# Loading all of x first, 1/rms through TensorE transposes, and padded stationaries by GpSimd, in a two-layer hybrid attention kernel

## The chip, the cores and the metric

One core of one Trainium2 chip runs the kernel in one launch. The metric is the device time of an execution in microseconds (us), the median of several runs. TensorE (PE; its weight loads are PEld), VectorE (DVE), ScalarE (ACT), GpSimd (POOL) and SyncE (SP, which here issues every DMA) each work through a queue of their own in order, and wait for one another by semaphores. TensorE has two clock levels, 1.2 and 2.4 GHz; the profile gives the granted share, 1.00 being the higher.

## The reference, cut to what matters

Two layers over 16 learned meta tokens and 1024 tokens of width 1024, all in float32. Each layer computes from u = RMSNorm(h) one projection u @ w_in, and from it two attention groups:

```
u = rms_norm(h, norm_g)
dq, dk, dv, dz, fq, fk, fv, fz, f_logit = split(u @ w_in)
# four differential heads: two softmaxes of 64-wide q and k with rope, one 128-wide v
p   = softmax(q1 k1^T / 8) - lam * softmax(q2 k2^T / 8)          # causal
o_a = rms_norm(p @ v_a, subln_g) * (1 - lambda_init)              # norm over the 128 of a head
# eight FoX heads of 64: softmax(q k^T / 8 + c_q - c_k), c = cumsum(log_sigmoid(f_logit + b))
o_b = p_f @ v_f
h   = h + concat(o_a * silu(dz), o_b * silu(fz)) @ w_out
```

After the second layer comes a last RMSNorm, and the meta rows are dropped. The norm over a head (rms_norm with subln_g) is what sub_norm below computes.

## The kernel before, in words

**Numbers.** Float32 products are made of float32r pairs: a value is split into a high part (rounded) and a low part (the rest), so that a product takes three matmuls (high x high, low x high, high x low). XTh and XTl hold u transposed in that form; load_w (lines 289 to 313) loads a column of 128 of w_in in four pieces of 128 KB and lets GpSimd make both parts (lines 307 and 310).

**Order of the work.** First all of x is normalised and transposed (lines 926 to 958). Then, for each layer, eight units j run one after another, four differential and then four FoX units of two heads each: unit_proj projects k, q and v (proj, line 334, in three chunks of about 346 tokens), attend makes scores, probabilities and outputs block by block of 128 queries, unit_gate projects z and multiplies. The projection of unit j+1 is written after the attention of unit j, before sub_norm(j) and the gates. The output projection (line 1049) closes a layer. Every pool of tiles is a set of buffers that the planner assigns: it takes the program as written, works out an order for each engine's queue from its own estimates of duration, places all tiles in memory and adds the waits, those for the reuse of memory included. Where a pool gives no count, the planner chooses it.

**The start.** Block 0 is the 16 meta rows, blocks 1 to 8 are 128 tokens each; they are loaded in the order 1, 0, 2, 3, ..., and after the fourth of them (W0 = 3) the four pieces of the first weight column are loaded. Groups of blocks, (1), (0, 2), (3, 4), (5, 6), (7, 8), are normalised: squares on ScalarE with a row sum, the chain of rsqrt on VectorE (lines 221 to 238, a start value and three Newton steps), and then rms_apply, x * r * g on VectorE (line 260), transposes on TensorE (line 275), a copy to XTh on ScalarE and the rest to XTl on VectorE (line 286). Blocks 5, 6 and 7 (PG) go another way: GpSimd multiplies by g alone (line 954), and a matmul against a diagonal of r scales and transposes at once (line 277).

**Differential units.** A block of 128 queries has two softmaxes, m = 0 and 1, over the two halves of the 128 partitions. The low part of the queries is used against both halves of k in one matmul, so it needs a stationary whose other half is zero: low_queries (lines 647 to 656) copies the half it needs, 64 partitions by 128, into one of two zeroed buffers qz by a DMA (named XTl<-ql in the trace, since the buffers lie in XTl's tile), two for each block, 68 blocks in all. finish_o leaves in U.vr the sums of squares of the outputs. sub_norm (lines 888 to 902) makes 1/rms of them in U.vr[:, 1], one column for each block of queries, one row for each query, while the outputs OT have queries along the free axis. So it writes the columns to DRAM (rr), loads them back as a row sent to all partitions (bc), and multiplies:

```
dma(row[NM:].rearrange("(b p) -> p b", p=P), U.vr[:, 1, 1:9])
bc = st("bc")
dma(bc[:, tq:], bcast_rows(row[tq:], P))
nc.vector.scalar_tensor_tensor(out=OT[:, tq:], in0=OT[:, tq:], scalar=gsc[...], in1=bc[:, tq:], ...)
```

Of the kernel before, what the change touches and what calls it, by code (L numbers as in the profile page):

```python
# [12 lines left out]
F32 = mybir.dt.float32  # L13
# [6 lines left out]
P = 128  # L20
NM = 16
# [6 lines left out]
PADC = (272, 544, 1056)  # L28
CSW = 1060
# [6 lines left out]
ECL = ((272, 4),)  # L36
# [4 lines left out]
W0 = 3  # L41
ON_POOL = ()
SPL_POOL = ()
GRPS = ((1,), (0, 2), (3, 4), (5, 6), (7, 8))
# [8 lines left out]
VPB = 2  # L53
STB = 3
NQZ = 2
PMB = 4
OTB = 2
CKB2 = 2
# [20 lines left out]
PG = (5, 6, 7)  # L79
# [37 lines left out]
def hybrid_kernel(ctx: ExitStack, tc: tile.TileContext, x, meta, norm_g, w_in, b_forget,  # L117
# [12 lines left out]
    sm = ctx.enter_context(tc.tile_pool(name="sm", bufs=6))  # L130
# [27 lines left out]
    def et(name, w=L):  # L158
        for i, (wmax, nb) in enumerate(ECL):
            if w <= wmax:  # L160
                return big.tile([P, wmax], F32, name=name, tag=f"es{i}" if i else "es", bufs=nb or None)
        return big.tile([P, LE], F32, name=name, tag="e", bufs=NE or None)
# [5 lines left out]
    cst = const.tile([P, max(CSW, P + 96 + MW // 2)], F32, name="cst")  # L168
# [21 lines left out]
    rr = [[dr.tile([L], F32, name=f"rr{i}_{j}") for j in range(4)] for i in range(DEPTH)]  # L190
# [50 lines left out]
    def rms_stats(hbs, junk, eng):  # L241

        ss = sm.tile([P, 4, 4], F32, name="ss", tag="ss", bufs=3)
# [19 lines left out]
    def put_ut(b, u, on_pool=False, r=None):  # L263

        t0, n = blk(b)
        if r is not None:
            dg = ptp.tile([P, P], F32, name="dg", tag="pm")
            nc.vector.tensor_scalar(out=dg[:n, :n], in0=ident[:n, :n], scalar1=r[:n], scalar2=None, op0=ALU.mult)
# [75 lines left out]
    def load_v01(l):  # L344
# [4 lines left out]
        wf = wp.tile([P, KT, 8], F32, name="wf", tag="wf", bufs=1)  # L349
# [16 lines left out]
    def proj_v01(l, his, los):  # L366
        Vs = [vp.tile([P, NB, 2, P], F32R, name="V", tag="V") for _ in range(2)]
        Vms = [vp.tile([96, 2, P], F32R, name="Vm", bufs=2) for _ in range(2)]
        vpre[l] = (Vs[1], Vms[1])

        mm = big.tile([P, 384], F32R, name="mm", tag="ck", bufs=CKB2 or None).rearrange("p (k c) -> p k c", k=KT)
# [8 lines left out]
        vm = big.tile([P, 384], F32, name="vm", tag="ck", bufs=CKB2 or None)[0:NM, :NV]  # L380
# [8 lines left out]
        fn = sm.tile([P, 8, NB], F32, name="fn", tag="fn", bufs=1)  # L389
        fm = sm.tile([NM, 8], F32, name="fm", tag="fm", bufs=1)  # L390
# [23 lines left out]
    def forget(l):  # L414
# [49 lines left out]
    def unit_proj(l, j, U, tabs):  # L464
# [113 lines left out]
        Vm = vp.tile([96, 2, P], F32R, name="Vm", bufs=2)  # L578

        def evv(ps, t0, n):  # L580
            vr = big.tile([P, 384], F32, name="vr", tag="ck", bufs=CKB2 or None)
            nc.scalar.activation(vr[:, :n], ps[:, :n], AF.Copy, scale=1.0 if diff else 0.5)
            late.append(lambda: transpose_v(vr, t0, n))
# [44 lines left out]
    def unit_gate(l, U, from_dram):  # L628
# [9 lines left out]
        def evz(ps, t0, n):  # L638
            gt = big.tile([P, 384], F32, name="gt", tag="ck", bufs=CKB2 or None)
# [7 lines left out]
    def low_queries(U, t):  # L647

        if not U.diff:
            return [U.Qb[m][:, t:t + P] for m in range(2)]  # L650
        qz = qzs[nqz[0] % NQZ]
        nqz[0] += 1
        for m in range(2):
            h = slice(64 * m, 64 * m + 64)
            dma(qz[h, m, :], U.ql[h, t:t + P])
        return [qz[:, m, :] for m in range(2)]

    def scores(U, m, i, low):
# [7 lines left out]
        s = sm.tile([P, 8], F32, name="sst", tag="sst", bufs=SSB or None)  # L666
# [93 lines left out]
    def split_meta(U, ps, n):  # L760
        pm = ptp.tile([96, 256], F32R, name="pm")
# [21 lines left out]
    def attend_meta(U):  # L783

        s = sm.tile([P, 8], F32, name="sst", tag="sst", bufs=SSB or None)
# [102 lines left out]
    def sub_norm(U):  # L888
# [84 lines left out]
    for l in range(DEPTH):  # L973
# [78 lines left out]
        def out_open(b):  # L1052
# [8 lines left out]
            ss = sm.tile([P, 4, 4], F32, name="ss", tag="ss", bufs=3)  # L1061
# [100 lines left out]
```

## Time and profile before

| | |
|---|---|
| median of three timed runs | 1522.74 us (1522.72 to 1524.1) |
| the profiled execution | 1519.45 us, span 1517.7 us from its first to its last instruction |
| TensorE / its weight loads busy | 1426.1 us (94%) / 1353.4 us (89%) |
| VectorE, ScalarE, GpSimd busy | 966.1 (64%), 697.7 (46%), 581.4 us (38%) |
| mean granted clock of TensorE | 0.975 |
| DMA | 128.37 MB, mean 85 GB/s |

A profile shows one execution. An engine's busy time counts the instructions, not its waits; a wait is put down to whatever released it last. Rows of a timeline give the start, the length, the engine and line, what is written from what is read, and in brackets how long the engine was idle before and what ended that. SPq rows are SyncE's DMA issues, not the transfers.

### The profile page before, as it was taken

What the parts mean: (1) busy time and instruction counts of PE and PEld (TensorE: products, weight loads), DVE (VectorE), ACT (ScalarE), POOL (GpSimd) and SP (SyncE); (2) the same over time, 40 slices, a digit from 0 to 9 for tenths busy, and PEclk for the clock granted to TensorE, in tenths of its full rate; (3) what the DMA queues carried; (4) which work ended last, traced back from release to release, by engine and by line L of the source; (5) the groups of instructions that cost most, each with busy time, mean ns of one, the idle gap of its engine ahead of it and who ended that gap; (6) DMA issues with size and microseconds to landing.
All of it is one profiled execution on the core that took longest, in us unless ns stands there. A gap on an engine that the chain in (4) does not pass through costs nothing.

```text
span 1517.7 us, 26880 instructions
## 1 busy us (share of the span) xinstructions
PE 1426.1 (94%) x9218; PEld 1353.4 (89%) x9218; DVE 966.1 (64%) x2729; ACT 697.7 (46%) x1729; POOL 581.4 (38%) x985
## 2 busy tenths in 40 slices
PE   3999988989899999999999998989898999999997
PEld 3998878989899999997789998889798999999886
DVE  6558684948465756575655686677566466756653
ACT  4236443626444655465323554445344455555521
POOL 6514243523344444464005233343333454535500
PEclk7999999999999999999999999999999999999999
DMA  8325232444133324356424244233433223244632
GB/s 191 66 51 76 33 96 47 87 55 93 25 101 65 62 50 65 93 148 183 135 102 96 40 68 73 55 76 64 61 70 81 68 50 82 45 83 122 208 132 84
DMA packets 132761, 128.37 MB, mean 85 GB/s; under 512 B 26192, under 2 KB 112336, under 8 KB 132624
## 3 DMA queue, kind: packets, MB, share of 16 engines
q1 hardware_dynamic: 132624, 126.65, 38.2%
q8 instruction: 73, 1.20, 0.3%
q14 instruction: 64, 0.52, 0.1%
HBM read 75.15 MB, written 21.57 MB: 64 GB/s over the span
## 4 chain that ended last, share of the span: by engine, by line
PE 69%; DMA 11%; DVE 10%; issue 4%; ACT 3%; POOL 2%; SPq 1%; DVEq 0%; ACTq 0%; POOLq 0%
PE pj L334 34%; PE pss L1049 4%; PE pj L1049 4%; DMA wraw<-in_w_in_dram 3%; PE pss L671 3%; PE pss L673 3%; PE pt L846 3%; PE pj L399 3%; PE po L780 2%; PE po L781 2%; DVE E L677 2%; DMA hb<-in_x_dram 1%; DMA bc<-rr 1%; DVE k L501 1%; PE po L778 1%
## 5 line engine op out<-in xcount | busy, mean ns | idle before, releaser
L334 PE MATMUL pj<-XTh,whi 128*128 128x346 f32 (+5 forms) x1392 | 456.4, 331 | 15.4 <-POOL whi L307 13.6
L334 PE MATMUL pj<-XTl,whi 128*128 128x346 f32 (+5 forms) x1392 | 454.5, 327 | 6.0 <-DVE XTl L286 6.0
L334 PE MATMUL pj<-XTh,wlo 128*128 128x346 f32 (+5 forms) x1392 | 455.5, 328 | 1.7 <-POOL wlo L310 1.7
L684 ACT ACTIVATE E<-E,sst 128x144 f32<-128x144 f32 (+7 forms) x256 | 202.1, 790 | 197.0 <-DVE sst L677 185.3
L334 PEld LDWEIGHTS pj<-XTh,whi 128*128 128x128 f32 x1392 | 265.6, 192 | 19.6 <-POOL whi L307 15.5
L334 PEld LDWEIGHTS pj<-XTl,whi 128*128 128x128 f32 x1392 | 266.1, 191 | 7.4 <-DVE XTl L286 6.4
L334 PEld LDWEIGHTS pj<-XTh,wlo 128*128 128x128 f32 x1392 | 266.5, 192 | 4.5 <-POOL wlo L310 3.6
L307 POOL TENSOR_SCALAR whi<-wraw 128x256 fp32r<-128x256 f32 x232 | 110.1, 475 | 346.4 <-DMA wraw<-in_w_in_dram 315.6
L310 POOL TENSOR_TENSOR wlo<-wraw,whi 128x256 fp32r<-128x256 f32 x232 | 181.0, 781 | 114.8 <-PE pj L334 97.7
L755 DVE TENSOR_TENSOR ptl<-pt,pth 128x512 fp32r<-128x512 f32 (+1 forms) x240 | 147.4, 633 | 52.5 <-ACT pth L754 47.0
L671 PE MATMUL pss<-k,qa 128*128 128x400 f32 (+7 forms) x448 | 154.1, 347 | 10.7 <-DVE sst L677 8.6
L754 ACT CAST pth<-pt 128x512 fp32r<-128x512 f32 (+1 forms) x240 | 122.7, 546 | 85.0 <-PE pt L846 29.8
L677 DVE CUSTOM_DVE_ANT_0 E<-pss,cst 128x400 f32<-128x400 f32 (+7 forms) x256 | 123.9, 491 | 40.6 <-PE pss L673 34.2
L701 POOL TENSOR_SCALAR E<-E,sst 128x400 f32<-128x400 f32 (+7 forms) x128 | 97.2, 762 | 136.2 <-DVE sst L700 121.2
L677 DVE CUSTOM_DVE_ANT_0 E<-pss,cst,sst 128x264 f32<-128x264 f32 (+2 forms) x192 | 112.1, 584 | 36.9 <-PE pss L673 31.9
L671 PEld LDWEIGHTS pss<-k,qa 128*128 128x128 f32 x448 | 86.0, 192 | 16.9 <-DVE sst L677 13.2
L846 PE MATMUL pt<-cst,E 128*128 128x128 f32 x576 | 89.8, 274 | 0.5 <-DVE sst L677 0.5
L780 PE MATMUL po<-pth,V 128*128 128x256 f32 x320 | 84.0, 286 | 0.6 <-POOL pth L865 0.6
L781 PE MATMUL po<-ptl,V 128*128 128x256 f32 x320 | 82.7, 287 | 0.0
L673 PE MATMUL pss<-k,XTl 128*128 128x400 f32 (+6 forms) x224 | 73.4, 334 | 4.0 <-DMA XTl<-ql 4.0
L494 POOL TENSOR_TENSOR sw<-sw,sin 128x694 f32<-128x694 f32 (+3 forms) x32 | 50.1, 1570 | 65.0 <-DMA sw<-raw 51.3
L673 PE MATMUL pss<-k,q 68*128 68x400 f32 (+6 forms) x224 | 72.8, 328 | 0.0
(337 smaller groups left out, 2881.3 us busy)
## 6 DMA issues: line engine op xcount, KB each, us to landing
wraw<-in_w_in_dram SPq DMA_DIRECT2D x256, 128.0 KB
hb<-in_x_dram SPq DMA_DIRECT2D x16, 512.0 KB
wor<-in_w_out_dram SPq DMA_DIRECT2D x64, 128.0 KB
XTl<-ql SPq DMA_DIRECT2D x136, 32.0 KB
sw<-raw SPq DMA_DIRECT2D x48, 86.8 KB
ms<-OT SPq DMA_DIRECT2D x8, 520.0 KB
k<-k SPq DMA_DIRECT2D x16, 260.0 KB
h<-hb SPq DMA_DIRECT2D x8, 512.0 KB
```

Of the source, the lines that this page charges most:

```text
L310: nc.gpsimd.tensor_tensor(out=lo, in0=raw, in1=hi.bitcast(F32), op=ALU.subtract)
L334: nc.tensor.matmul(ps[:, :n], lhsT=w, rhs=xx[:, k, t0:t0 + n], start=(cnt == 0), stop=(cnt == 23))
L671: nc.tensor.matmul(ps[:, :nn], lhsT=U.Qa[m][:, t:t + P], rhs=U.K1[m][:, c0:c0 + nn], start=True, stop=False)
L673: nc.tensor.matmul(ps[:, :nn], lhsT=low[m], rhs=U.Kb[m][:, c0:c0 + nn], start=False, stop=True)
L677: nc.vector.tensor_tensor_reduce(out=E[:, c0:c0 + n], in0=ps[:, :n], in1=k, scale=-1.0, scalar=s[:, c - 1:c] if CHN and c else -NEG, op0=A ...
L684: nc.scalar.activation(E[:, :W], E[:, :W], AF.Exp, scale=-1.0, bias=lo, accum_out=s[:, 4:5])
L754: nc.scalar.copy(hi, ps)
L755: nc.vector.tensor_tensor(out=lo, in0=ps, in1=hi.bitcast(F32), op=ALU.subtract)
L780: nc.tensor.matmul(o[:, :256], lhsT=U.V[:, kb, hd, :], rhs=hi, start=False, stop=False)
L781: nc.tensor.matmul(o[:, :256], lhsT=U.V[:, kb, hd, :], rhs=lo, start=False, stop=last)
L846: nc.tensor.transpose(ps[:, (2 * a + b) * P:(2 * a + b + 1) * P], PP[:, k0:k0 + P], ident)
L1049: nc.tensor.matmul(ps, lhsT=xx[:, k, m0:m0 + P], rhs=wo[k][w][:, c], start=(k == 0 and i == 0), stop=(k == KT - 1 and i == 2))
```

## The change

Five things are changed at once.

1. The start: the first weight column is loaded after all nine blocks of x (W0 = 8); the groups are (0, 1, 2), (3, 4, 5), (6, 7, 8); PG is empty, so every block goes through rms_apply on VectorE and plain transposes.
2. sub_norm: no DRAM. For each block of queries TensorE transposes the column of 1/rms spread over 128 columns (a broadcast operand), which gives a PSUM tile with the row in every partition; VectorE multiplies from there, four blocks at a time.
3. low_queries: a GpSimd copy (multiplication by one) instead of the DMA, into one of three buffers instead of two.
4. The pool sm and the tags es, ck and subn go: their tiles become rings at fixed places in the tile cst, with as many slots as there were buffers, handed out in the order of the program. Two tiles mm move to the tag pth.
5. Paddings: PADC 264, 528, 1056, 2112 (264 is the quarter of 1056), some tiles widened from 96 or 16 to 128 partitions; the number of buffers of the pool of V is left to the planner (VPB = 0).

```diff
-PADC = (272, 544, 1056)
-CSW = 1060
+PADC = (264, 528, 1056, 2112)
-W0 = 3
+W0 = 8
-GRPS = ((1,), (0, 2), (3, 4), (5, 6), (7, 8))
+GRPS = ((0, 1, 2), (3, 4, 5), (6, 7, 8))
-VPB = 2
+VPB = 0
-NQZ = 2
+NQZ = 3
-PG = (5, 6, 7)
+PG = ()
...
-    sm = ctx.enter_context(tc.tile_pool(name="sm", bufs=6))
...
+    small = [("es", 4, 272), ("ck", 2, 384), ("subn", 2, 36), ("sst", SSB, 8), ("ss", 3, 16), ("fn", 1, 64), ("fm", 1, 8), ("wf", 1, 64)]
+    cst = const.tile([P, P + 96 + MW // 2 + sum(n * w for _, n, w in small)], F32, name="cst")
+    rings, at = {}, P + 96 + MW // 2
+    for nm, n, w in small:
+        rings[nm] = [at, n, w, 0]
+        at += n * w
+
+    def slot(nm):
+        r = rings[nm]
+        c = r[0] + r[3] % r[1] * r[2]
+        r[3] += 1
+        return cst[:, c:c + r[2]]
...
-            dma(qz[h, m, :], U.ql[h, t:t + P])
+            nc.gpsimd.tensor_scalar(out=qz[h, m, :], in0=U.ql[h, t:t + P].bitcast(F32), scalar1=1.0, scalar2=1.0,
+                                    op0=ALU.mult, op1=ALU.mult)
...
-        row = rr[U.l][U.j]
-        if U.l == 0:
-            dma(row[0:NM].rearrange("(p b) -> p b", b=1), U.vr[0:NM, 1, 0:1])
-        dma(row[NM:].rearrange("(b p) -> p b", p=P), U.vr[:, 1, 1:9])
-        bc = st("bc")
-        dma(bc[:, tq:], bcast_rows(row[tq:], P))
-        nc.vector.scalar_tensor_tensor(out=OT[:, tq:], in0=OT[:, tq:], scalar=gsc[:, U.l, U.j:U.j + 1],
-                                       in1=bc[:, tq:], op0=ALU.mult, op1=ALU.mult)
+        for t0, n, cols in ((0, NM, (0,)), (NM, 4 * P, (1, 2, 3, 4)), (NM + 4 * P, 4 * P, (5, 6, 7, 8))):
+            if t0 < tq:
+                continue
+            ps = pt()
+            w = min(n, P)
+            for i, c in enumerate(cols):
+                nc.tensor.transpose(ps[:, w * i:w * i + w], U.vr[0:w, 1, c:c + 1].to_broadcast([w, P]), ident[0:w, 0:w])
+            o = OT[:, t0:t0 + n]
+            nc.vector.scalar_tensor_tensor(out=o, in0=o, scalar=gsc[:, U.l, U.j:U.j + 1], in1=ps[:, :n],
+                                           op0=ALU.mult, op1=ALU.mult)
```

## Rows read from the trace of the kernel before

**Rows 1.** The page, busy time by engine.

```profile
PE 1426.1 (94%) x9218; PEld 1353.4 (89%) x9218; DVE 966.1 (64%) x2729; ACT 697.7 (46%) x1729; POOL 581.4 (38%) x985
```

**Rows 2.** Windows by stage: length, PE, PEld, DVE, ACT, POOL busy (count), clock, DMA, GB/s.

```profile
97.00:430.00 333.00, 302.74 (x1944) 287.10 (x1943) 226.86 (x670) 155.34 (x407) 120.65 (x193) 0.96 0.36 66
430.00:850.00 420.00, 418.43 (x2712) 393.32 (x2711) 255.03 (x721) 196.03 (x491) 166.16 (x295) 1.00 0.40 95
850.00:1157.00 307.00, 280.25 (x1832) 269.76 (x1831) 211.14 (x595) 145.06 (x358) 110.01 (x181) 0.97 0.38 68
```

**Rows 3.** Windows of the first 20 us.

```profile
0.00:10.00 10.00, 6.68 (x44) 6.49 (x45) 3.54 (x16) 5.35 (x9) 3.08 (x14) 1.00 0.82 271
10.00:20.00 10.00, 3.62 (x22) 2.87 (x20) 5.50 (x15) 3.29 (x7) 4.82 (x6) 0.62 1.03 98
```

**Rows 4.** Timeline, 406 to 421 us: start, length, engine, line, tiles, [idle before, releaser].

```profile
406.15 0.17 DVE L237 SCALAR_TENSOR_TENSOR vr__3863<-vr__3863 128x9 f32<-128x9 f32 x1
...
406.35 1.04 SPq L141 DMA_DIRECT2D rr<-vr__3863  x2
...
414.19 0.35 SPq L141 DMA_DIRECT2D bc<-rr  x1
414.60 0.93 SPq L301 DMA_DIRECT2D wraw<-in_w_in_dram  x2
418.97 1.30 DVE L901 SCALAR_TENSOR_TENSOR OT<-OT,gsc,bc 128x1040 f32<-128x1040 f32 x1 [7.52 <-DMA bc<-rr]
...
420.77 0.58 PE L758 MATMUL po<-pm,Vm 96*128 96x256 f32 x1 [7.39 <-DVE pm L770]
```

**Rows 5.** Waits of the engines: total us, times, longest.

```profile
DVE OT L901 <- DMA bc<-rr: 61.8, 8, 11.5
...
PE pss L673 <- DMA XTl<-ql: 4.0, 2, 3.8
```

**Rows 6.** Windows of 20 us around eight gaps: one, and the sum.

```profile
408.00:428.00 20.00, 12.61 (x71) 12.18 (x70) 9.28 (x26) 6.00 (x14) 7.62 (x11) 0.83 0.34 108
...
sum 160.00, PE 122.36 PEld 114.52 DVE 84.02 ACT 51.13 POOL 61.20; mean PE 15.30 PEld 14.32 DVE 10.50 ACT 6.39 POOL 7.65
```

**Rows 7.** Timeline of the start, by engine.

```profile
9.25 0.18 ACT L249 ACTIVATION_READ_ACCUMULATOR u<-hb 16x1 f32 x1
...
19.62 0.78 SPq L141 DMA_DIRECT2D hb<-in_x_dram  x1
...
33.02 2.34 DVE L354 TENSOR_TENSOR vwl<-wf,vwh 128x32 fp32r<-128x32 f32 x1
...
39.05 0.66 PE L334 MATMUL pj<-XTl,whi 128*128 128x348 f32 x1 [6.03 <-DVE XTl L286]
...
53.54 0.69 DVE L286 TENSOR_TENSOR XTl<-pt,XTh 128x512 fp32r<-128x512 f32 x1 [1.47 <-ACT XTh L285]
```

**Rows 8.** The page, groups of instructions: busy us, mean ns, idle before.

```profile
L307 POOL TENSOR_SCALAR whi<-wraw 128x256 fp32r<-128x256 f32 x232 | 110.1, 475 | 346.4 <-DMA wraw<-in_w_in_dram 315.6
L310 POOL TENSOR_TENSOR wlo<-wraw,whi 128x256 fp32r<-128x256 f32 x232 | 181.0, 781 | 114.8 <-PE pj L334 97.7
...
L846 PE MATMUL pt<-cst,E 128*128 128x128 f32 x576 | 89.8, 274 | 0.5 <-DVE sst L677 0.5
```

**Rows 9.** Waits of GpSimd, 97 to 430 us, then 850 to 1155 us.

```profile
POOL whi L307 <- DMA wraw<-in_w_in_dram: 96.2, 37, 9.5
...
POOL whi L307 <- DMA wraw<-in_w_in_dram: 120.0, 38, 11.8
```

**Rows 10.** Groups of GpSimd's instructions by form.

```profile
L954 POOL TENSOR_TENSOR u<-hb,gb 128x1024 f32<-128x1024 f32 x3 | 7.0, 2348 | 0.0
...
L701 POOL TENSOR_SCALAR E<-E,sst 128x144 f32<-128x144 f32 x16 | 6.2, 385 | 10.4 <-DVE sst L700 6.2 <-DVE vr__3863 L237 4.2
...
L820 POOL MEMSET vr__2876<- 128x36 f32 x1 | 0.1, 128 | 10.3 <-DMA rr<-vr__997 10.3
```

**Rows 11.** Waits of SyncE's queue.

```profile
SPq L141 <- PE pss L673: 94.8, 40, 19.8
```

More of the change, by code (lines that the diff above doesn't have):

```diff
@@ L35 @@
 NE = 4
-ECL = ((272, 4),)
 TLS = True
@@ L158, in et @@
     def et(name, w=L):
-        for i, (wmax, nb) in enumerate(ECL):
-            if w <= wmax:
-                return big.tile([P, wmax], F32, name=name, tag=f"es{i}" if i else "es", bufs=nb or None)
+        if w <= 272:
+            return slot("es")
         return big.tile([P, LE], F32, name=name, tag="e", bufs=NE or None)
@@ L189, in hybrid_kernel @@
     fx = dr.tile([8, L], F32, name="fx")
-    rr = [[dr.tile([L], F32, name=f"rr{i}_{j}") for j in range(4)] for i in range(DEPTH)]
     nlam = const.tile([P, DEPTH], F32, name="nlam")
@@ L241, in rms_stats @@
     def rms_stats(hbs, junk, eng):
-        ss = sm.tile([P, 4, 4], F32, name="ss", tag="ss", bufs=3)
+        ss = slot("ss").rearrange("p (a b) -> p a b", a=4)
         m = len(hbs)
@@ L266, in put_ut @@
         if r is not None:
-            dg = ptp.tile([P, P], F32, name="dg", tag="pm")
+            dg = ptp.tile([P, 2 * P], F32, name="dg", tag="pm")[:, 0:P]
             nc.vector.tensor_scalar(out=dg[:n, :n], in0=ident[:n, :n], scalar1=r[:n], scalar2=None, op0=ALU.mult)
@@ L348, in load_v01 @@
         his, los = room("vwh"), room("vwl")
-        wf = wp.tile([P, KT, 8], F32, name="wf", tag="wf", bufs=1)
+        wf = slot("wf").rearrange("p (k c) -> p k c", k=KT)
         dma(wf, w_in[l, :, 4096:4104].rearrange("(k p) c -> p k c", p=P))
@@ L367, in proj_v01 @@
         Vs = [vp.tile([P, NB, 2, P], F32R, name="V", tag="V") for _ in range(2)]
-        Vms = [vp.tile([96, 2, P], F32R, name="Vm", bufs=2) for _ in range(2)]
+        Vms = [vp.tile([P, 2, P], F32R, name="Vm")[0:96] for _ in range(2)]
         vpre[l] = (Vs[1], Vms[1])
-        mm = big.tile([P, 384], F32R, name="mm", tag="ck", bufs=CKB2 or None).rearrange("p (k c) -> p k c", k=KT)
+        mm = ptp.tile([P, 512], F32R, name="mm", tag="pth", bufs=PHB or None)[:, :384].rearrange("p (k c) -> p k c", k=KT)
         nc.gpsimd.memset(mm.bitcast(F32), 0.0)
@@ L379, in proj_v01 @@
                                  start=(k == 0 and i == 0), stop=(k == KT - 1 and i == 1))
-        vm = big.tile([P, 384], F32, name="vm", tag="ck", bufs=CKB2 or None)[0:NM, :NV]
+        vm = slot("ck")[0:NM, :NV]
         nc.scalar.copy(vm, ps[32:32 + NM, :NV])
@@ L577, in unit_proj @@
         V4 = V.rearrange("p b a (c d) -> p b (a c) d", d=64)
-        Vm = vp.tile([96, 2, P], F32R, name="Vm", bufs=2)
+        Vm = vp.tile([P, 2, P], F32R, name="Vm")[0:96]
         def evv(ps, t0, n):
-            vr = big.tile([P, 384], F32, name="vr", tag="ck", bufs=CKB2 or None)
+            vr = slot("ck")
             nc.scalar.activation(vr[:, :n], ps[:, :n], AF.Copy, scale=1.0 if diff else 0.5)
@@ L638, in evz @@
         def evz(ps, t0, n):
-            gt = big.tile([P, 384], F32, name="gt", tag="ck", bufs=CKB2 or None)
+            gt = slot("ck")
             nc.scalar.activation(gt[:, :n], ps[:, :n], AF.Tanh, scale=0.5)
@@ L665, in scores @@
         chs = [(c * n0, n0 if c < nch - 1 else W - c * n0) for c in range(nch)]
-        s = sm.tile([P, 8], F32, name="sst", tag="sst", bufs=SSB or None)
+        s = slot("sst")
         E = et("E", W)
@@ L760, in split_meta @@
     def split_meta(U, ps, n):
-        pm = ptp.tile([96, 256], F32R, name="pm")
+        pm = ptp.tile([P, 256], F32R, name="pm")
         if U.diff:
@@ L783, in attend_meta @@
     def attend_meta(U):
-        s = sm.tile([P, 8], F32, name="sst", tag="sst", bufs=SSB or None)
+        s = slot("sst")
         pm2 = ptp.tile([P, 256], F32, name="pm2", tag="pm")[0:16, 0:192].rearrange("p (m c) -> p m c", m=2)
@@ L817, in attend @@
         if U.diff:
-            U.vr = sm.tile([P, 3, 12], F32, name="vr_", tag="subn", bufs=2)
+            U.vr = slot("subn").rearrange("p (a b) -> p a b", a=3)
             if U.l == 0:
@@ L1033, in hybrid_kernel @@
         if l == 0:
-            mm = big.tile([P, 384], F32R, name="mm", tag="ck", bufs=CKB2 or None).rearrange("p (k c) -> p k c", k=KT)
+            mm = ptp.tile([P, 512], F32R, name="mm", tag="pth", bufs=PHB or None)[:, :384].rearrange("p (k c) -> p k c", k=KT)
             nc.gpsimd.memset(mm.bitcast(F32), 0.0)
@@ L1060, in out_open @@
             u = st("u")[:, :D]
-            ss = sm.tile([P, 4, 4], F32, name="ss", tag="ss", bufs=3)
+            ss = slot("ss").rearrange("p (a b) -> p a b", a=4)
             return b, hb, u, ss
```

12 lines of the change are left out of this document (5 added, 7 removed).

## The prediction

> **What bounds the kernel now.** I read the page first: TensorE is busy for 94% of the span, so only its gaps, its slow stretches and its own work can move the time much [rows 1]. The windows by stage then say where the gaps are [rows 2]. In the stage of the FoX units (430 to 850 us, with the output projection of the first layer) TensorE is busy 418.43 of 420 us at full clock: nothing to win there. The two stages of the differential units (j below 4, one per layer) leave 333 - 302.74 = 30.3 us and 307 - 280.25 = 26.8 us idle, at granted clocks of 0.96 and 0.97. At the start TensorE is busy only 6.68 and 3.62 us of the first two stretches of 10 us [rows 3]. Those three stretches are what counts.
>
> In the differential stages I then looked at the timeline of single gaps. Eight of them stand at the eight calls of sub_norm, and one shows how they come about [rows 4]. VectorE finishes 1/rms at 406.32; SyncE issues the stores to rr, waits in its own queue until they have landed, issues the broadcast load bc only at 414.19, and the weights that stand behind it at 414.60. VectorE in its turn stands in front of the multiply of line 901 until 418.97, although a piece that TensorE needs (line 770) is queued right behind it; TensorE resumes at 420.77. Over the eight calls VectorE stands still for 61.8 us there [rows 5]. Eight windows of 20 us around these places hold 122.36 us of TensorE work in 160, so 37.6 us idle, and their clocks (0.88, 0.91, 0.91, 0.83, 0.91, 0.91, 0.83, 0.91 in order of time; one window and the sum stand in the rows) fall short of one by 0.91 in all, which times 20 us is another 18.2 us of full speed: the engine stood idle and came back at the lower of its two levels, 1.2 GHz, for a while. Together some 56 us are lost around sub_norm [rows 6].
>
> **The change: the start.** SyncE's queue now loads x in between the weights; the last block of x is issued only at 19.62. In 0 to 10 us the queue moved 271 GB/s, in 10 to 20 us 98 GB/s, with the DMA engines full in the second stretch and nearly so (0.82) in the first: the weights' loads fill the engines with fewer bytes [rows 3, 7]. The projection goes on steadily only at 39.05, and the last block of XTl is written at 54.23 [rows 7].
> After it, x, gb and the meta rows (4.8 MB) come first and are in at about 18.5 us at 271 GB/s; the 0.5 MB of the first weight column follow at 98 GB/s by about 24 us, and GpSimd splits the last piece in 0.475 + 0.78 us (lines 307 and 310) [rows 8]. On VectorE the group of blocks 0 to 2 can start when its third square is done at 9.43 us [rows 7]: a chain of eleven short operations of about 0.2 us, 2.2 us; its products, 1.3 us each (line 901 is the same operation on 1040 columns) [rows 4]; its subtractions, 0.69 us for half a block [rows 7]. With that, block 3, the last one that the first chunk of 348 columns needs, is split at about 24 us, and block 8 at about 39. So TensorE starts its first chunk at 24 to 26 us in place of 39.05. 39 - 25 = 14 us gained. The diagonal products of blocks 5 to 7 become plain transposes on TensorE, and GpSimd loses three products of 2.35 us (line 954) to VectorE; both lie in the times above. Bounds: 5 us if the weights of the second and third column take most of it back, 18 us if the split keeps up with the loads. I take -14.
>
> **1/rms by transposes.** Away go 8 loads bc, 12 stores to rr, VectorE's 61.8 us of standing, and SyncE's waits for the landing, so the weights behind (as at 414.60) go out 5 to 8 us sooner. What is late next is just those weights: GpSimd waits 96.2 + 120.0 us for them in these two stages [rows 9], and a part of that stays. Of the 56 us I therefore count three quarters: -41 (bounds -19, a third, and -56). Added are 36 + 32 = 68 transposes of one column spread over 128. The trace has no such operand; the nearest row is the transpose of 128x128, 576 of them in 89.8 us, so 0.156 us each in a row and 0.274 us for one alone [rows 8]. They stand on the engine that bounds: 68 x 0.156 = +10.6 (up to 18.6, and down to 0 if they fall into gaps). The multiply becomes two instructions of 512 columns from PSUM instead of one from SBUF, 2 x 0.69 against 1.30 us: nothing. The added wait is TensorE's, for the chain of 1/rms. Behind the transposes in TensorE's queue stand the next projection and the next scores, and for those wait VectorE and ScalarE. If each call stood for the whole chain it would be 8 x 2.2 = 18 us, the upper bound, and 0 is the lower; I take +3, since other TensorE work lies between the last attention product and the transposes and VectorE's queue is no transfer that comes late by itself.
>
> **Padded stationaries by GpSimd.** 136 transfers XTl<-ql of SyncE become 136 GpSimd instructions of 64x128. They lie between 0.128 us (a memset of 36 columns) and 0.475 us (line 307, 256 columns); the nearest is line 701 at 144 columns, 0.385 us, and I take 0.35: 48 us more on an engine that is busy 120.65 + 110.01 us in these 640 [rows 2, 8, 10]. That lies beside TensorE's work unless a copy stands behind a wait in GpSimd's queue. Now the transfer stands likewise behind SyncE's waits (94.8 us for L673 of TensorE alone) [rows 11], and TensorE lost 4.0 us by it in the whole kernel, in two places [rows 5]; three buffers instead of two give more lead. I take +4 (-1 to +40; of the 4.0 us, 3.8 are already among the eight gaps).
>
> **One tile of rings, other paddings, V's buffers left to the planner.** Number of slots and their order stay; addresses, some waits for reuse and the planned order change. No row prices that. A reuse wait that shows, of a memset of vr for the store from an older vr, was 10.3 us on GpSimd [rows 10]. I take 0, from -10 to +10.
>
> **The sum.** -14 - 41 + 10.6 + 3 + 4 = -37.4. The profiled execution took 1519.45 us, of which the span is 1517.7; 1519.45 - 37.4 = 1482. The median of the timed runs is 3.3 us above the profiled one, so 1485.
>
> **A rule that speaks against it.** A VectorE subtraction of only 32 columns (line 354) took 2.34 us at 33.02 us, as long as a GpSimd product of line 954, 2.35 us [rows 7, 10]. The Trainium skill, GPSIMD Engine Reference, section Specifications, says that GpSimd shares its SBUF interfaces with VectorE and contends with VectorE instructions that have two SBUF inputs or run in a two-port mode; by that rule, the trace agrees. The three products taken from GpSimd would then be a gain of up to 7 us at the start, and every copy added a possible hold on VectorE: rival (d).
>
> **The rivals.**
> (a) The weights take the place. GpSimd's 216 us of waiting for them are more than what SyncE loses at the eight landings, so they are late elsewhere too. If half of what I count back stays lost, 1485 + 20 = 1505. Against: at 414.60 and 418.97 weights and VectorE were let go by one round trip.
> (b) All comes back: -56 and -18, transposes half hidden (+5), neither +3 nor +4: 1519.45 - 69 + 3.3 = 1454.
> (c) GpSimd's queue decides, and the kernel is slower. A copy stands behind a line 307 that waits for its weights, the scores wait for the copy, TensorE and then VectorE for the scores. GpSimd waits so for 216 of 638 us, 34%, in 75 waits of 2.9 us [rows 9]. If a third of the 68 pairs of copies met one in full, 23 x 2.9 = 67 us: 1485 - 4 + 67 = 1548. The sign turns from 14 pairs on (41 us). Against: the same stood on SyncE, and cost 4.0 us.
> (d) VectorE is held by every copy, 136 x 0.35 = 48 us, all of it passed on: 1485 + 48 = 1533. Against: VectorE has 226.86 of 333 and 211.14 of 307 us of work there [rows 2], so some 200 us of room.
> (e) The change does not do at the start what it says: weights still go out between the blocks of x, and the 14 us are not won: 1499. Against: what goes out late now, the last block at 19.62, has weights ahead of it in the written order too.
>
> **How the numbers follow.** Forecast 0.55 (its own range 1470 to 1500); (a) 0.16, (b) 0.12, (c) 0.06, (d) 0.04, (e) 0.07. The range takes in (a), (e) and the nearer part of (b): 1457 to 1510; (c), (d) and the edges of (a) and (b) are left out, under 0.2. Within 0.2% (3 us) no change can be told by measurement here; (c) with some 14 pairs ends there. From (c) and (d) slower is 0.08, the same 0.03, and faster 0.89.
>
> **What would show it.** No VectorE wait for a bc; TensorE's gaps at the eight places below 12 us in sum and a clock of 0.97 or more in windows around them; transposes in sub_norm near 0.16 us; the steady projection from between 22 and 30 us on; GpSimd copies of about 0.35 us and TensorE's wait for them below 8 us in all. The prediction is wrong if TensorE idles more than 45 us in the two differential stages together, or if the first projection goes on steadily only after 35 us.

## The result, and the profile of the changed kernel

The median of four timed runs is 1500.05 us (1496.26 to 1502.85), against 1523.16 us for the kernel before on the same chip: a ratio of 0.9846 with a 95% interval of 0.9822 to 0.987. The forecast was 1485, its range 1457 to 1510. The profiled execution took 1498.74 us, span 1497.1, where the sum of the prediction gives 1482. The sign and the range hold, the point is 15 us too low, and the parts of the sum are further off than their total.

The page, busy time by engine (as [rows 1]):

```profile
PE 1419.0 (95%) x9262; PEld 1348.8 (90%) x9262; DVE 955.3 (64%) x2721; ACT 699.9 (47%) x1729; POOL 627.8 (42%) x1118
```

TensorE stands for 1497.1 - 1419.0 = 78.1 us, before for 1517.7 - 1426.1 = 91.6. Half of its busy time in stretches at the lower clock is what that clock costs: 12.8 us, before 25.2. The rest is its work at full clock, 1406.2 against 1400.9. So -13.5 - 12.4 + 5.3 = -20.6 us of span.

Windows by stage, with the bounds moved so that they lie as far from the same work as in [rows 2] (2 and 6 us after the v projection of the layer ends, 29 and 24 us after its last sums of squares):

```profile
110.00:428.00 318.00, 304.28 (x2025) 292.89 (x2024) 230.30 (x681) 158.60 (x411) 145.17 (x261) 0.98 0.33 57
428.00:855.00 427.00, 418.26 (x2667) 388.53 (x2666) 252.09 (x722) 193.82 (x489) 170.76 (x300) 1.00 0.38 92
855.00:1137.00 282.00, 272.32 (x1859) 264.85 (x1858) 212.74 (x598) 145.95 (x354) 131.84 (x237) 1.00 0.34 60
```

Read the lengths. The two differential stages went from 333 + 307 = 640 to 318 + 282 = 600 us, and TensorE stands in them for 13.7 + 9.7 = 23.4 us in place of 57. But everything ahead of the first one now takes 110 us in place of 97, and the stretch between them, which ends with the v projection of layer 1, 427 in place of 420. So +13 - 15 + 7 - 25 - 0.6 (the rest) = -20.6.

**Around sub_norm.** Eight windows of 20 us around the multiplies, one and the sum (as [rows 6]):

```profile
327.00:347.00 20.00, 17.68 (x110) 17.14 (x110) 15.14 (x63) 8.55 (x30) 8.63 (x17) 0.91 0.30 50
...
sum 160.00, PE 153.79 PEld 148.02 DVE 122.26 ACT 70.29 POOL 81.25; mean PE 19.22 PEld 18.50 DVE 15.28 ACT 8.79 POOL 10.16
```

The 37.6 us of idle time have become 160 - 153.79 = 6.2, and the clock is 1.00 in seven windows and 0.91 in the one shown: 1.8 us in place of 18.2. The groups of instructions (busy us, mean ns | idle before, and its releasers) tell what it costs (as [rows 8, 10]):

```profile
L314 POOL TENSOR_SCALAR whi<-wraw 128x256 fp32r<-128x256 f32 x232 | 106.7, 460 | 186.7 <-DMA wraw<-in_w_in_dram 156.6 <-PE pj L341 14.0 <-PE po L785 6.3
...
L662 POOL TENSOR_SCALAR XTl<-ql 64x128 fp32r<-64x128 f32 x136 | 50.8, 379 | 120.4 <-PE pss L681 95.6 <-DVE ql L508 8.1 <-PE pss L800 8.1
...
L911 DVE SCALAR_TENSOR_TENSOR OT<-OT,gsc,pt 128x512 f32<-128x512 f32 (+1 forms) x20 | 12.1, 637 | 0.1
L909 PE MATMUL pt<-cst 128*128 128x128 f32 (+1 forms) x68 | 9.3, 272 | 1.4 <-DVE cst L244 1.4
```

L909 are the 68 transposes: 9.3 us in all, 0.137 us each in a row. The multiplies of L911 wait for nothing, where line 901 waited 61.8 us. L662 are the copies. GpSimd's wait for weights halved, from 315.6 to 156.6 us; but GpSimd now also stands 120.4 us before the copies, so that alone does not show that weights come earlier. What counts is TensorE's wait for a split weight, before and after (us, times, longest):

```profile
PE pj L334 <- POOL whi L307: 13.6, 4, 6.9
```

```profile
PE pj L341 <- POOL whi L314: 3.9, 6, 1.0
```

**The start.** Windows of the start (as [rows 3], and one more):

```profile
0.00:10.00 10.00, 6.53 (x40) 6.34 (x40) 1.52 (x11) 5.86 (x10) 3.31 (x14) 1.00 0.80 270
10.00:20.00 10.00, 4.28 (x24) 3.85 (x24) 8.13 (x24) 7.03 (x16) 0.00 (x0) 0.83 0.97 181
20.00:45.00 25.00, 2.55 (x13) 2.55 (x13) 10.18 (x21) 2.28 (x4) 13.52 (x20) 0.50 0.64 109
```

From 20 to 45 us TensorE works for 2.55 us. The timeline says why (as [rows 7]):

```profile
3.12 2.19 SPq L137 DMA_DIRECT2D hb<-in_x_dram  x4
...
10.69 3.67 DVE L267 SCALAR_TENSOR_TENSOR u<-hb,cst,gb 16x1024 f32<-16x1024 f32 x3
...
11.74 4.72 SPq L302 DMA_DIRECT2D wraw<-in_w_in_dram  x4
16.50 8.72 SPq L302 DMA_DIRECT2D cst<-in_w_in_dram  x4
25.27 0.86 SPq L137 DMA_DIRECT2D cos<-in_rope_cos_dram  x1
...
30.97 0.61 SPq L137 DMA_DIRECT2D hb<-in_x_dram  x1
...
37.75 1.06 ACT L256 ACTIVATE u<-hb 128x1024 f32<-128x1024 f32 x1 [19.19 <-DMA hb<-in_x_dram]
...
41.11 4.15 DVE L267 SCALAR_TENSOR_TENSOR u<-hb,cst,gb 128x1024 f32<-128x1024 f32 x3
42.45 2.82 PE L282 MATMUL pt<-cst,u 128*128 128x128 f32 x12 [25.62 <-DVE u L267]
...
44.92 0.64 PE L341 MATMUL pj<-XTh,whi 128*128 128x348 f32 x1
```

Eight blocks of x are issued first, the ninth at 30.97 us, behind eight loads of weights and the tables of the rope. ScalarE waits 19.19 us for it, VectorE's chain and products follow, TensorE stands for 25.62 us, and the projection begins at 44.92. The ninth is block 5: in the written program the blocks 1 to 5 take tiles of one tag, "e", that has four buffers, so block 5 gets the buffer of block 1 and its load must wait until VectorE has multiplied block 1 (L267: the three products of the first group are done at 14.36 us). The rest, until 30.97, is SyncE's order: the planner gives that time to the weights, whose eight issues alone keep SyncE from 11.74 to 25.22 us. The new groups put blocks 3, 4 and 5 into one chain of rsqrt, so two blocks that are there wait for the one that isn't.

**Two new waits.** Waits of the engines (us, times, longest):

```profile
POOL XTl L662 <- PE pss L681: 95.6, 33, 20.6
...
PE pss L799 <- DMA qa<-qa: 5.9, 1, 5.9
...
PE pss L679 <- DMA qa<-qa: 5.0, 2, 4.8
```

The two waits of TensorE stand one in each layer, before the first scores of the layer; the first on the timeline:

```profile
80.84 0.28 PE L406 MATMUL pj<-vwh,XTl 128*128 128x264 f32 x1
82.83 1.56 ACT L515 CAST qa<-raw 64x694 fp32r<-64x694 f32 x2 [0.90 <-ACT Vm L394]
83.63 1.28 SPq L137 DMA_DIRECT2D qa<-qa  x2
...
87.03 0.35 PE L799 MATMUL pss<-k,qa 128*128 128x16 f32 x1 [5.91 <-DMA qa<-qa]
```

L406 is the v projection, of which 144 of 192 matmuls are still to be done at 80.84. In TensorE's queue the first scores (L799) now stand in the middle of it, ahead of what is ready, and the queries they need are copied at 82.83 and sent to their place at 83.63. Afterwards TensorE runs at 0.50 from 84.9 to 91.7 us. Before, TensorE never waited for qa<-qa.

### The profile page after: what moved, and what is told of

It is laid out like the page before. It is cut to its first block, busy times and chain, and to the rows that moved or that the text cites. A ratio compares the mean times of both kernels' runs of the same rounds, so it can differ in the third digit from the quotient of the medians.

```text
span 1497.1 us, 26781 instructions
## 1 busy us (share of the span) xinstructions
PE 1419.0 (95%) x9262; PEld 1348.8 (90%) x9262; DVE 955.3 (64%) x2721; ACT 699.9 (47%) x1729; POOL 627.8 (42%) x1118
## 4 chain that ended last, share of the span: by engine, by line
PE 75%; DVE 8%; DMA 5%; SPq 4%; ACT 3%; issue 2%; POOL 2%; DVEq 0%; POOLq 0%; ACTq 0%
PE pj L341 36%; PE pss L1059 5%; PE pj L1059 5%; PE pss L679 4%; PE pt L854 4%; PE pss L681 4%; SPq L137 3%; PE pj L406 2%; PE po L788 2%; PE po L789 2%; DMA sw<-raw 2%; DMA wraw<-in_w_in_dram 2%; DVE E L685 2%; PE pt L1059 1%; POOL sw L501 1%
## 5 line engine op out<-in xcount | busy, mean ns | idle before, releaser
L685 DVE CUSTOM_DVE_ANT_0 E<-pss,cst 128x456 f32<-128x456 f32 (+6 forms) x384 | 210.2, 557 | 68.6 <-PE pss L681 42.1
L692 ACT ACTIVATE E<-E,cst 128x400 f32<-128x400 f32 (+2 forms) x192 | 172.4, 898 | 137.2 <-DVE cst L685 130.5
L314 POOL TENSOR_SCALAR whi<-wraw 128x256 fp32r<-128x256 f32 x232 | 106.7, 460 | 186.7 <-DMA wraw<-in_w_in_dram 156.6
L762 ACT CAST pth<-pt 128x512 fp32r<-128x512 f32 (+1 forms) x240 | 126.9, 543 | 92.9 <-PE pt L854 34.5
L709 POOL TENSOR_SCALAR E<-E,cst 128x400 f32<-128x400 f32 (+2 forms) x96 | 83.8, 874 | 132.3 <-DVE cst L708 102.3
L662 POOL TENSOR_SCALAR XTl<-ql 64x128 fp32r<-64x128 f32 x136 | 50.8, 379 | 120.4 <-PE pss L681 95.6
```

Source lines behind the costliest of these rows:

```text
L685: nc.vector.tensor_tensor_reduce(out=E[:, c0:c0 + n], in0=ps[:, :n], in1=k, scale=-1.0, scalar=s[:, c - 1:c] if CHN and c else -NEG, op0=A ...
L692: nc.scalar.activation(E[:, :W], E[:, :W], AF.Exp, scale=-1.0, bias=lo, accum_out=s[:, 4:5])
L762: nc.scalar.copy(hi, ps)
```

## The experiments

Three sets, the first two on one chip and the third on another, with the kernel before beside each (medians 1518.2, 1519.33 and 1515.95 us; with the run above they differ by up to 0.5%, so ratios to before are compared across sets). Such a ratio has an error of its own: the changed kernel and after_null (below), which have the same order, took 1500.05 and 1501.24 us, but have ratios of 0.9846 and 0.9892, since the kernel before took 1523.16 us beside the one and 1515.95 beside the other. The parts 1 to 3 were tried on top of parts 4 and 5 (rings, paddings, V's buffers to the planner), which give them room in memory.

**First set: one part at a time.** "rings" is the kernel before with parts 4 and 5 alone, and NQZ = 2; the others add one part each to it.

```diff
 # rings_start
+W0 = 8
+GRPS = ((0, 1, 2), (3, 4, 5), (6, 7, 8))
+PG = ()
 # rings_transp: the transposes of sub_norm in place of rr and bc
+                nc.tensor.transpose(ps[:, w * i:w * i + w], U.vr[0:w, 1, c:c + 1].to_broadcast([w, P]), ident[0:w, 0:w])
 # rings_copies
+NQZ = 3
-            dma(qz[h, m, :], U.ql[h, t:t + P])
+            nc.gpsimd.tensor_scalar(out=qz[h, m, :], in0=U.ql[h, t:t + P].bitcast(F32), scalar1=1.0, scalar2=1.0, ...)
```

Expected of rings: 

> The kernel before with the rings, paddings and V's planned buffers alone (parts 4 and 5). Theory A (the fixed places only move addresses; the gain comes from the transposes, the loss against the forecast from the start): 1523 us, between 1518 and 1528, the eight gaps at sub_norm still there with some 37 us. Theory B (better packing gives a part of the gain): 1512 or less. Theory C (false waits between slots of one tile cost): 1530 or more.

Expected of rings_start: 

> Rings and the new start (parts 1, 4, 5). Theory A (one block of x has no buffer until an earlier block is normalised, is therefore issued behind the weights and rope tables, and its group, for which TensorE's queue waits first, starts only at about 39 us): 3 us slower than the rings alone, TensorE's gap in the first 50 us about 25 us in one piece, steady projection from about 47 us. Theory B (the start wins what was forecast, and something else loses it): 10 to 14 us faster than the rings alone.

Expected of rings_transp: 

> Rings and 1/rms by transposes (parts 2, 4, 5). Theory A (both the standing of VectorE and of SyncE's queue were the round trip): 30 to 35 us faster than the rings alone, about 1490, the gaps at sub_norm below 8 us in sum. Theory B (late weights take the place): 15 to 20 us faster, with TensorE waiting for whi in the second layer as before.

Expected of rings_copies: 

> Rings and padded stationaries by GpSimd (parts 3, 4, 5). Theory A (the copy looks early to the planner, which then puts the first scores ahead of the rest of the v projection, and they wait for the transfer qa<-qa): two gaps of about 5 us at the first scores of each layer, 5 to 12 us slower than the rings alone. Theory B (copies cost nothing, the two gaps come from elsewhere): within 4 us of the rings alone, no wait for qa<-qa over 1 us.

**Second set: one part undone**, and a buffer of its own for block 5.

```diff
 # no_newstart: W0, GRPS and PG as before; no_transp: rr and bc again
 # no_copies
-NQZ = 3
+NQZ = 2
-            nc.gpsimd.tensor_scalar(out=qz[h, m, :], ...)
+            dma(qz[h, m, :], U.ql[h, t:t + P])
 # buf5
-    htags = [("st", ST)] + [("e", NE)] * 5 + [("st", ST)] * 2 + [("ot", OTB)]
+    htags = [("st", ST)] + [("e", NE)] * 4 + [("ql", STB)] + [("st", ST)] * 2 + [("ot", OTB)]
...
-        hb = big.tile([P, L], F32, name="hb", tag=tg, bufs=nb or None)[:, :D]
+        hb = (stk if tg == "ql" else big).tile([P, L], F32, name="hb", tag=tg, bufs=nb or None)[:, :D]
```

Expected of no_newstart: 

> The changed kernel with the start of before (parts 2 to 5). Theory A (the new start loses some 3 us by its late block of x, and the gain of 8 us that rings_start showed over rings is the planner's new order elsewhere): within 5 us of the changed kernel, some 0.985 of the kernel before, start segment 3 us shorter, first steady projection at about 39 us. Theory B (parts add up as measured on top of the rings: start -8): 8 us slower than the changed kernel, 0.990.

Expected of no_copies: 

> The changed kernel with the padded stationaries by DMA into two buffers again (parts 1, 2, 4, 5). Theory A (parts add up: copies -5.5): 0.988 to 0.990 of the kernel before, that is 5 us slower than the changed kernel. Theory B (copies matter little once sub_norm no longer blocks SyncE): within 3 us of the changed kernel.

Expected of no_transp: 

> The changed kernel with the round trip through DRAM again (parts 1, 3, 4, 5). Theory A (parts add up: transposes -17 to -20): 0.998 of the kernel before, 17 to 20 us slower than the changed kernel, eight gaps at sub_norm with about 35 us. Theory B (copies and start had already taken what the transposes would give): less than 10 us slower.

Expected of buf5: 

> The changed kernel with one more place for x: the fifth of the blocks 1 to 5, which share four buffers, gets a buffer of its own from the tag ql. Theory A (that block has no buffer until block 1 is normalised, goes out behind weights and rope tables at about 31 us, and TensorE's queue waits for its group): all of x issued by about 6 us, the gap of 25 us shrinks below 12, first steady projection before 34 us, 12 to 16 us faster than the changed kernel. Theory B (the weights behind x are the limit): gap above 18 us, less than 5 us faster.

What was measured; the gaps are TensorE's of 3 us and more in the profiled execution (number and sum), read from the timeline: at the start, before the first scores of a layer for qa<-qa, and in the differential stages:

| kernel | new start | transposes | copies | median us | ratio to before, 95% | start | qa<-qa | differential |
|---|---|---|---|---|---|---|---|---|
| before | | | | | 1 | 2: 18.7 | 0 | 6: 30.3 |
| rings | | | | 1529.4 | 1.0068 (1.0045 to 1.0091) | 2: 17.8 | 1: 3.2 | 7: 32.9 |
| rings_start | x | | | 1521.06 | 1.0013 (0.9998 to 1.0028) | 1: 26.8 | 0 | 7: 25.4 |
| rings_copies | | | x | 1523.93 | 1.0042 (1.0023 to 1.0061) | 2: 18.6 | 0 | 7: 35.1 |
| no_transp | x | | x | 1530.14 | 1.0076 (1.0049 to 1.0103) | 1: 26.1 | 1: 4.7 | 8: 33.5 |
| rings_transp | | x | | 1512.72 | 0.9958 (0.9942 to 0.9974) | 1: 15.3 | 2: 11.8 | 1: 3.3 |
| no_copies | x | x | | 1517.45 | 0.9995 (0.9981 to 1.0009) | 1: 26.2 | 2: 12.1 | 1: 3.3 |
| no_newstart | | x | x | 1503.03 | 0.9898 (0.9875 to 0.9922) | 1: 15.5 | 2: 10.9 | 0 |
| changed | x | x | x | 1500.05 | 0.9846 (0.9822 to 0.987) | 1: 25.6 | 2: 10.7 | 0 |

Two columns sort the kernels cleanly, whatever else is in them. With the round trip through DRAM there are six to eight gaps in the differential stages, 25 to 35 us, with the transposes none or one. In no_transp VectorE waits again (a row of its waits):

```profile
DVE OT L910 <- DMA bc<-rr: 59.9, 8, 8.7
```

And with the new start the gap at the start is 26 us, without it 15 to 19: loading "all x first" with four buffers for five blocks makes it 7 to 11 us longer. The projection of the first q and k ends only 2.3 to 2.8 us later in each pair, since later waits shrink. The waits for qa<-qa are 10.7 to 12.1 us in all four kernels with transposes, and 0 to 4.7 in the others; that the copies bring them, as I had thought, fell: rings_copies has none.

The times sort less well, and most of the theories missed them. rings came out 11.2 us above the kernel beside it, nearest to theory C; rings_start 8.3 us below rings, which neither theory said, though A's gap came; rings_transp 16.7 us below, B's time with A's gaps; rings_copies 5.5 us below, without A's waits. no_newstart is 3 us above the changed kernel by the medians (A) and 0.5% by the ratios (B); no_copies is 17 us above it, more than three times what either theory said, and no_transp 30 us, where A said 17 to 20.

Averaged over the four pairs, transposes are worth -1.26% (-19 us), copies -0.43%, the new start -0.09% (with after_null's ratio for the changed kernel -1.14, -0.32 and +0.02%); but single pairs run from -0.2 to -2.3%, -1.5 to +0.6% and -0.6 to +0.4%. Either the parts need one another, or the planner's new order for each program moves the time by itself.

buf5 did at the start what it should: the gap is 11.7 us, the projection of q and k ends at 61.3 us, 12.0 earlier than in the changed kernel. Yet its median is 1498.9 us (0.9867, 0.9848 to 0.9886), the changed kernel's within both spreads. The timeline of buf5 shows where the 12 us went:

```profile
52.15 0.46 ACT L491 ACTIVATE raw<-pj 128x346 f32<-128x346 f32 x1 [5.25 <-PE pj L341]
...
56.69 4.75 SPq L308 DMA_DIRECT2D wraw<-in_w_in_dram  x2
61.53 2.51 SPq L137 DMA_DIRECT2D sw<-raw  x4
...
65.66 0.88 DVE L500 TENSOR_TENSOR raw<-raw,cos 128x694 f32<-128x694 f32 x1 [18.40 <-DMA sw<-raw]
...
69.09 1.56 ACT L515 CAST k<-raw 64x694 fp32r<-64x694 f32 x2 [16.48 <-DVE raw L502]
...
82.12 1.77 SPq L137 DMA_DIRECT2D qa<-qa  x2
...
85.77 0.35 PE L799 MATMUL pss<-k,qa 128*128 128x16 f32 x1 [16.64 <-DMA qa<-qa]
```

The first keys are projected and copied at 52.6 us; their halves are exchanged for the rope by a transfer (sw<-raw) that is issued at 61.53, behind loads of weights on SyncE; ScalarE then waits 16.48 us for the rope, the queries come after it, and the first scores, still ahead of most of the v projection in TensorE's queue, wait 16.64 us. They start at 85.77, against 87.03 in the changed kernel, and the v projection ends at 108.2 and 108.1 us. The order of lines on TensorE is the same in the two but for four of 3437 runs of equal lines, so nothing else is compared here.

**Third set: the two theories apart.** First, the order: the low copies of unit 0 are multiplied by a column of ones that VectorE makes after the v projection, and their matmul goes first, so that the first scores can't stand ahead of it. after_order is this in the changed kernel, buf5_order in buf5. Second, a null edit in rings and in the changed kernel: 16 warming matmuls at the very start in place of 20.

```diff
 # after_order, buf5_order
+        nc.vector.tensor_scalar(out=onec[:, l:l + 1], in0=fn[:, 0, NB - 1:NB], scalar1=0.0, scalar2=1.0, op0=ALU.mult, op1=ALU.add)
...
-            nc.gpsimd.tensor_scalar(out=qz[h, m, :], in0=U.ql[h, t:t + P].bitcast(F32), scalar1=1.0, scalar2=1.0,
+            nc.gpsimd.tensor_scalar(out=qz[h, m, :], in0=U.ql[h, t:t + P].bitcast(F32),
+                                    scalar1=onec[h, U.l:U.l + 1] if U.j == 0 else 1.0, scalar2=1.0,
...
+            pair = [(U.Qa[m][:, t:t + P], U.K1[m]), (low[m], U.Kb[m])]
+            for a, (w, x) in enumerate(pair[::-1] if U.j == 0 else pair):
 # rings_null, after_null
-WARM = 20
+WARM = 16
```

Expected of after_order: 

> The changed kernel, with the first scores of each layer held back until the v projection is done: the low copies of unit 0 are multiplied by a column of ones that VectorE makes after the v projection, and for unit 0 the matmul with the low copy comes first of the two. Theory A (the two gaps of 5.9 and 4.8 us, in which TensorE stands for the transfer qa<-qa, are a loss of order in TensorE's queue, and the low clock after them is lost with them): both gaps go, the v projection of layer 0 ends 6 to 10 us earlier than the 108.1 us of the changed kernel, and the whole is 8 to 15 us faster than the changed kernel, near 1488 us. Theory B (the scores come later and VectorE and ScalarE start the softmax later, so the same time is lost in the attention behind): the gaps go, the v projection ends earlier, but the first differential stage is longer by as much and the time is within 4 us of the changed kernel.

Measured: 1493.12 us, 0.9835 (0.9809 to 0.9861). The v projection ends at 98.7 us, 9.4 earlier; both waits for qa<-qa are gone. Against after_null of the same set (1501.24) that is -8.1 us: theory A, at its lower end. But the profiled executions of the two show something of theory B as well. The v projection takes 23.6 us in each layer, in after_null 32.4 and 31.9. From its end to the output projection, layer by layer, after_null and then after_order:

```profile
107.95:676.23 568.28, 553.09 (x3765) 535.48 (x3765) 386.86 (x1168) 295.12 (x751) 264.68 (x488) 1.00 0.35 69
846.26:1394.65 548.39, 538.09 (x3723) 528.41 (x3723) 373.64 (x1077) 286.34 (x688) 253.09 (x472) 1.00 0.34 68
```

```profile
98.65:670.84 572.19, 553.38 (x3772) 536.37 (x3771) 387.72 (x1169) 294.59 (x749) 264.12 (x496) 1.00 0.35 68
834.84:1392.10 557.26, 540.83 (x3729) 529.41 (x3729) 380.72 (x1082) 286.38 (x690) 258.30 (x480) 1.00 0.33 66
```

Of the 17.1 us won in the two v projections, 3.9 and 8.9 are lost again in the attention behind them, where TensorE stands 3.6 and 6.1 us longer. (These two executions lie closer than the medians, 1494.94 and 1497.36 us.)

Expected of buf5_order: 

> The same holding back of the first scores, in the kernel where block 5 of x has a buffer of its own (its start was 12 us shorter and was given back at a gap of 16.6 us before qa<-qa). Theory A (given back only there): the gap goes, the v projection ends at 92 to 98 us in place of 108.2, and the time is 20 to 30 us below that kernel's, near 1473 us. Theory B (the start's gain does not reach the end, since another wait takes it: weights, or VectorE's softmax behind): the v projection ends later than 102 us or the first differential stage grows, and the time is within 5 us of that kernel's 1498.9 us.

Measured: 1480.23 us, 0.9758 (0.9736 to 0.9779). The v projection ends at 85.9 us, earlier than either theory said, and the time is 18.7 us below buf5's, which ran on the other chip (16.5 by the ratios): theory A, a little smaller than expected. The stretch from 60 to 110 us in the changed kernel, buf5, after_order and buf5_order:

```profile
60.00:110.00 50.00, 43.65 (x311) 43.35 (x310) 20.64 (x52) 13.38 (x36) 18.24 (x23) 0.93 0.21 52
```

```profile
60.00:110.00 50.00, 32.32 (x236) 32.02 (x235) 20.92 (x52) 12.89 (x35) 18.33 (x23) 0.80 0.21 51
```

```profile
60.00:110.00 50.00, 50.00 (x366) 49.67 (x365) 23.45 (x70) 15.72 (x48) 19.33 (x27) 1.00 0.24 56
```

```profile
60.00:110.00 50.00, 46.84 (x348) 45.83 (x347) 30.67 (x89) 20.01 (x59) 25.44 (x33) 1.00 0.32 70
```

In buf5 TensorE works for 32.32 us there and the clock is 0.80; with the first scores held back it is 46.84 us at 1.00. With that in both, the buffer for block 5 is worth 1493.12 - 1480.23 = 12.9 us, the 12.7 us that the end of the first q and k moves (73.3 to 60.6). buf5_order beats both kernels.

Expected of rings_null: 

> The kernel before with the rings, paddings and V's buffers alone, and 16 instead of 20 warming matmuls at the very start, which nothing waits for: an edit worth under 1 us by itself. Theory A (what the parts interact by is scatter of the planned order: any edit moves the gaps): it differs from the kernel with the rings alone (1529.4 us) by 4 to 10 us either way, with other gaps. Theory B (the planned order is stable and the interactions are the parts' own): within 3 us of it, with the same gaps at the same places.

Measured: 1540.29 us, 1.0152 (1.0133 to 1.0171), 10.9 us above rings, with eight gaps of 3 us and more in the differential stages at other places; laid side by side as well as they can be, the two orders of lines on TensorE share 2738 of 3488 runs. Scatter, theory A, a little more than its 4 to 10 us.

Expected of after_null: 

> The changed kernel with 16 instead of 20 warming matmuls at the very start: an edit worth under 1 us by itself. Theory A (scatter of the planned order): 4 to 10 us away from the changed kernel's 1500 us, either way, with other gaps. Theory B (stable order): within 3 us, with the 25.6 us gap at the start and both waits for qa<-qa where they were.

Measured: 1501.24 us, 0.9892 (0.9867 to 0.9916), 1.2 us above the changed kernel, and the lines of TensorE, VectorE, ScalarE and GpSimd come in exactly the same order. Theory B: here the order is stable.

So an edit that means nothing moves rings by 11 us, because the planner finds another order, and leaves the changed kernel as it is. Of the pairs in the table only changed and no_newstart have nearly one order (3429 of 3437 runs of lines on TensorE; next come rings_transp and no_copies with 3391 of 3491). In that pair the new start as made is worth -3 us by the medians, -8 by the ratios and -1 with after_null's ratio for the changed kernel, so it can't be told from nothing. In the others an unknown part of the difference is the order. What rings, copies and transposes are worth each to within 10 us stays open, and why the transposes come with first scores inside the v projection too; that the transposes close the gaps of the differential stages, that the new start opens one, and that the waits for qa<-qa cost what after_order wins, some 8 us after what the attention gives back, does not.

## Why the prediction was right in total and wrong in its terms

**The start: -14 forecast, +3.4 measured to the end of the first q and k (69.9 to 73.3 us).** This step failed. "Block 3 is split at about 24 us, and block 8 at about 39" took the loads to follow one another because the queue could move them; it did not ask which buffer each block gets. Five tiles in a tag of four buffers mean that one block waits for a product of VectorE and then for all that SyncE has queued in between. Rival (e), "weights still go out between the blocks of x", is what happened. That its price, 1499, is so near the median of 1500.05 is luck, since the terms behind the start were off too. What I held against it was wrong: the last block at 19.62 [rows 7] is the one load of x there that waits for VectorE and ScalarE, so it too had to stand behind a product. Even with a buffer for the block the term was too large: in buf5_order the first q and k end at 60.6 us, 9.3 earlier than in the kernel before, not 14. The 12.9 us of that buffer are counted from the late start of the changed kernel.

**What is late next at the start: not in the sum.** The v projection ends at 108.1 in place of 95.2 us: beyond the 3.4 us, 5.9 are the wait for qa<-qa, and of the other 3.6 the low clock after it is 2.1. It is not the late block that shows there: no_newstart, with the start of before, ends its first q and k 2.8 us earlier than the changed kernel, waits 7.3 us for qa<-qa and ends the v projection at 108.4. In layer 1 the same wait takes 4.8 us, and from the end of the output projection to the end of the v projection it is 58.2 us, before 50.2. So -14 became +13 at the start, and layer 1 added +7.

**The holes round sub_norm: -41 forecast, -47.8 measured** (31.4 idle, 16.4 low clock). Three quarters of 56 were counted, six sevenths came. Rival (a), that weights would take the place, did not come: TensorE's wait for split weights fell from 13.6 to 3.9 us.

**The transposes: +10.6 forecast, +9.3 measured.** The row of L846 was the right neighbour: 0.156 us, against 0.137. **The wait for 1/rms: +3 forecast, 1.4 measured.**

**The copies: +4 forecast; no wait of TensorE for them in the profile after.** 0.35 us each was close to the mean of 0.379. They stand long behind the scores that still read their buffer (95.6 us in 33 waits), as rival (c) had it of GpSimd's queue, but TensorE's wait for the weights that are split behind them was only 3.9 us. Of rival (d) there is little: VectorE's instructions beside a copy are some 7 us longer in all than the same instructions beside an idle GpSimd (an estimate from the trace of the changed kernel), not 48, and VectorE's busy time fell from 966.1 to 955.3 us.

**Rings and paddings: 0 (-10 to +10) forecast.** Alone they gave +0.68% and, with the null edit, +1.52%, 10 and 23 us, all of it within what another order can do; in the changed kernel the term can't be told from its order.

In the differential stages the terms sum to -41 + 10.6 + 3 + 4 = -23.4; measured -40. Of these 16.6 us, 6.8 are sub_norm, 1.3 the transposes, 1.6 the wait for 1/rms and 4 the copies; 2.9 stay open. With 27 us too much hoped of the start and 7 of layer 1 not seen, 27 + 7 - 16.6 - 0.6 = 16.8, which is the distance from 1482 to 1498.74. That the range held is in part luck: errors of 34 us one way and 16.6 the other. Of the marks named ahead, those of sub_norm came true (6.2 us of gaps, clocks of 1.00 but for one of 0.91, no wait for bc); that of the start, "only after 35 us", said wrong: 44.92.

## What to carry to other kernels

A load moved ahead is early only if its buffer is free: count the tiles of a tag against its buffers, and a group that shares one chain starts with its last block. When a stage gets shorter, look at what is queued behind it in the fixed order: 12 us won at the start were all lost at a wait that stood ahead of ready work, and came back when that work was put first (though the attention behind took a part of what the new order won). Where a planner orders the queues, compare two kernels part by part only if their orders agree, and measure a null edit before believing differences below 1%.

## What the runs showed of the hardware

GpSimd and VectorE hold each other up. In the changed kernel, beside VectorE's three products of 128x1024 from 20.82 to 24.63 us, and again at 41.11:

```profile
20.82 3.81 DVE L267 SCALAR_TENSOR_TENSOR u<-hb,cst,gb 128x1024 f32<-128x1024 f32 x3
22.56 1.01 POOL L314 TENSOR_SCALAR whi<-wraw 128x256 fp32r<-128x256 f32 x1 [1.98 <-DMA wraw<-in_w_in_dram]
23.54 1.68 POOL L317 TENSOR_TENSOR wlo<-wraw,whi 128x256 fp32r<-128x256 f32 x1
25.27 0.41 POOL L314 TENSOR_SCALAR whi<-wraw 128x256 fp32r<-128x256 f32 x1
25.64 0.72 POOL L317 TENSOR_TENSOR wlo<-wraw,whi 128x256 fp32r<-128x256 f32 x1
...
45.18 0.72 DVE L361 TENSOR_TENSOR vwl<-cst,vwh 128x32 fp32r<-128x32 f32 x1
...
46.51 0.17 DVE L361 TENSOR_TENSOR vwl<-cst,vwh 128x32 fp32r<-128x32 f32 x1
```

A GpSimd instruction of 0.41 us takes 1.01 beside the products, one of 0.72 takes 1.68. The products pay as well, but less: three of them take 3.67 us at 10.69, while GpSimd stands, 3.81 beside these instructions and 4.15 at 41.11, beside two subtractions of GpSimd; the longer one of each three is the last, with 1.42 and 1.75 us in place of 1.27. A small VectorE subtraction of 0.17 us takes 0.72 while GpSimd finishes an instruction (until 45.85 us), as the 2.34 us in [rows 7] did. The copies range widely too:

```profile
L662 POOL TENSOR_SCALAR XTl<-ql x136: 288/297/1261, 85.6 to 1067.9; 64x128 fp32r<-64x128 f32 x136
```

(shortest, median, longest in ns.) Of the 136, 93 overlap a VectorE instruction that reads two tensors, and take 0.29 to 1.26 us; the other 43 take 0.29 to 0.32. The Trainium skill, GPSIMD Engine Reference, section Specifications, says that the two share SBUF interfaces and contend when VectorE has two SBUF inputs; the trace agrees, and shows that either side can pay.
